# A transformer layer in exact fp32: unread products at the start, earlier weight tiles, and lower parts of weights made by an accumulating DMA

## The chip, the cores and the metric

The kernel runs on one core of one Trainium2 chip. The metric is the device time of one execution in microseconds (us). A core has TensorE (PE, matrix products, with a weight load that overlaps them), VectorE (DVE), ScalarE (ACT), GpSimd (POOL) and SyncE (SP). On-chip data lies in SBUF with 128 partitions; products land in eight banks of PSUM. Transfers from HBM are issued from a queue of an engine and moved by 16 DMA engines that the core's queues share.

## What is computed

One layer of a diffusion backbone for 512 latent tokens with a prefix of 256 context tokens, width 1024, all in fp32:

```python
mod = silu(c) @ w_ada + b_ada            # six vectors of 1024; the same for c_ctx
h  = rms_norm(x, g_norm1) * (1 + sc1) + sh1
hc = rms_norm(ctx, g_norm1) * (1 + csc1) + csh1
aq, ak, av, dq, dk, dv, dz, da, db, ga, gd = split_cols(h @ w_in)
...
y_attn = window_ctx_attention(q_a, k_a, v_a, k_ac, v_ac, attn_sink)
o_dl, _, _ = bidir_delta(*dn_inputs(dq, dk, dv, da, db), s_cf, s_cb)
...
y = sigmoid(gate_a) * (y_a @ w_br_attn) + sigmoid(gate_d) * (y_d @ w_br_dn)
x_new = x + gt1 * (y @ w_out)
x_new = x_new + gt2 * (square(relu(norm2(x_new) @ w_mlp1)) @ w_mlp2)
```

Here `y_d` is the normalised output of a bidirectional gated delta rule times `silu(dz)`, and `norm2` the second modulated RMS norm.

## The kernel before

**Precision.** Every weight product is made of three fast products. `split` and `wload` turn an fp32 operand into an upper part (a copy rounded to the fast type) and a lower part (operand minus upper part); `mm3` (L266) adds upper times upper, upper times lower, and lower times upper, on lines 271, 272 and 273, into one PSUM bank. `gate_tiles` (L925) and `br_a` (L970) do the same inline.

**Weight tiles.** A weight tile is 128 x 1024 (512 KB), that is 128 output columns with all eight blocks of 128 inputs; tiles of the branch projections (`wbr`) are half as large. `wload` issues the load on SP's queue into a ring of raw buffers, tag `wr`, of NWR = 4. ACT copies the raw tile to the upper part (L262), and DVE subtracts it from the raw tile for the lower part (L263). The parts go either into the rings `wh` and `wl` of NWS = 2 buffers each, or into buffers of a hand-managed arena (shown as `m` in the profile).

There are three groups of tiles.

- Three *early* tiles of `w_in`, with arena buffers. They are loaded within the loop over the eight blocks of x (`kt`): two at kt = 0 and one at kt = 1. After each block is normalised, the products of that block with all early tiles are issued, so these tiles advance as blocks become ready.
- Sixty *late* tiles: 36 of `w_in`, 16 of `wbr`, 8 of `w_out`, in a fixed list `wq`. `wnext` hands out the tile that was prepared and starts the load of the next, so one tile is prepared ahead. They use the rings `wh` and `wl`.
- Sixty-four MLP tiles, loaded by `wload` with arena buffers, far ahead of their use.

The raw ring is also used by `late_mod` (L988): 32 tiles `wa` of modulation weights, which DVE multiplies and sums on line 990, 16 of them between 379 and 440 us and 16 around the start of the MLP.

**The start.** SP's queue first carries x, the context and the 16 tiles of modulation weights `wada1` in 512 KB loads. `ada(kt)` (L190, products on L198) needs two of these; `columns(kt)` (L209) has ACT copy its result (L212), PE reduce it (L217) and DVE write the modulation of block kt. Meanwhile ACT squares and DVE sums x and the context, PE adds over partitions with a matrix of ones (L247), and ACT makes the reciprocal root. `modulate` (L275) then makes the upper and lower part of a normalised block: DVE on L276, ACT on L277, DVE on L278. The results stay on chip for all later input tiles.

**The stages after.** Input tiles are woven with attention (to about 300 us), the delta rule's chunks and their triangular solve (to about 440), gate tiles, the delta branch's projection (534 to 556), `w_out` (556 to 602) and the MLP (from 602). Generators written by hand set the order of instructions within each engine's queue; a helper library adds the semaphores, and each engine runs its queue in order.

Of the kernel before, what the change touches and what calls it, by code (L numbers as in the profile page):

```python
# [8 lines left out]
F32 = mybir.dt.float32  # L9
F32R = mybir.dt.float32r  # L10
BF16 = mybir.dt.bfloat16
AF = mybir.ActivationFunctionType
ALU = mybir.AluOpType
# [1 line left out]
PSUM = bass.MemoryType.PSUM  # L15

NU = 167
NWR, NWS = 4, 2
FILL = 144, 28, 36, (8, 7, 3)
INV = 2, 12, 18, 0  # L20
QTS = 7, 5, 4, 7, 3, 6, 10, 7
# [1 line left out]
LEAD = 0  # L23
ATT = 32
NHALF = 3
AHEAD = 2
LATE = 6, 3, 0
NPL = ()
# [3 lines left out]
P = 128  # L32
D = 1024
KT = D // P
# [17 lines left out]
T_AK, T_AV, T_AQ, T_AB = 0, 1, 2, 6  # L52
T_DK, T_DV, T_DQ, T_DZ = 7, 11, 15, 19
# [41 lines left out]
def tile_layer(ctx: ExitStack, tc: tile.TileContext, I: dict, out: bass.AP, dbg=None):  # L95
    nc = tc.nc
    V, A, G, PE = nc.vector, nc.scalar, nc.gpsimd, nc.tensor
# [4 lines left out]
    sb = ctx.enter_context(tc.tile_pool(name="sb", bufs=1))  # L102
# [3 lines left out]
    def nm(s):  # L106
        uid[0] += 1
        return f"{s}_{uid[0]}"
# [3 lines left out]
    banks = Arena(lambda o, n: psum[:, o:o + n], 512, 8)  # L112
# [4 lines left out]
    alloc, bank = mem.get, lambda n=1: banks.get(n * 512)  # L117
# [10 lines left out]
    r32 = lambda ap: ap.bitcast(F32R)  # L128
# [23 lines left out]
    ones = const.tile([P, P], F32, name="ones")  # L152
# [27 lines left out]
        (eng or V).tensor_tensor(r32(lo), src, hi, op=ALU.subtract)  # L180


    scb = alloc(256)
    scond = scb.ap.rearrange("p (k v) -> p k v", k=KT)
    V.memset(scb.ap, 0.0)
# [4 lines left out]
    def ada(kt):  # L190


        rp_ = banks.get(512, True)
        for half in range(2):
            wb = alloc(1024)
            nc.sync.dma_start(out=wb.ap, in_=I["wada1"][kt, half])
            for g in range(4):
                PE.matmul(rp_[32 * g:32 * g + 32, :256], scond[:, half * 4 + g], wb[:, g * 256:(g + 1) * 256],  # L198
                          start=(half == 0), stop=(half == 1))
            wb.free()  # L200
        return rp_
# [7 lines left out]
    def columns(kt, rp_):  # L209

        rb_ = alloc(256)
        A.activation(rb_.ap, rp_[:, :256], AF.Copy)  # L212
        rp_.free()
        mp_ = banks.get(512, True)
        mp = mp_[:, 0:4].rearrange("p (h n) -> p h n", h=2)
        for half in range(2):
            PE.matmul(mp[:, half, :], rb_[:, half * P:(half + 1) * P], prm[:, 184:186], start=True, stop=True)  # L217
        rb_.free()

        V.tensor_scalar(modA[:, kt, :], mp[:, 0, :], bada1[:, kt:kt + 1], g1[:, kt:kt + 1], op0=ALU.add, op1=ALU.mult)  # L220
        V.tensor_scalar(modS[:, kt, :], mp[:, 1, :], bada[:, kt:kt + 1], None, op0=ALU.add)
        mp_.free()

    columns(0, ada(0))
    for k4 in range(KT // 4):
        nc.sync.dma_start(out=cs_[:, k4 * 1024:(k4 + 1) * 1024], in_=I["ctxT"][k4])
    xt = [xs_[:, k * SEQ:(k + 1) * SEQ] for k in range(KT)]
    ct_ = [cs_[:, k * CTX:(k + 1) * CTX] for k in range(KT)]
    rstd = alloc(768)
# [2 lines left out]
    for src, nt, n, r in ((xs_, 4, SEQ, rx), (cs_, 2, CTX, rc)):  # L232
        tot = None
        for i in range(nt):
            b = alloc(1024)
# [6 lines left out]
        w = 512  # L242
# [9 lines left out]
        act(r, r, AF.Exp, scale=-0.5)  # L252


    def wload(src, n=KT, bufs=None):
        raw = sb.tile([P, KT, P], F32, tag="wr", bufs=NWR, name=nm("wr"))[:, :n]
        nc.sync.dma_start(out=raw, in_=src)
        if bufs:
            hi, lo = (b.ap.rearrange("p (k c) -> p k c", k=KT) for b in bufs)
        else:  # L260
            hi, lo = (sb.tile([P, KT, P], F32, tag=t, bufs=NWS, name=nm(t))[:, :n] for t in ("wh", "wl"))
        A.activation(r32(hi), raw, AF.Copy)  # L262
        V.tensor_tensor(r32(lo), raw, hi, op=ALU.subtract)  # L263
        return r32(hi), r32(lo)

    def mm3(acc, w, xs, start=True, stop=True, ks=None):  # L266
        ks = list(range(len(xs))) if ks is None else ks
        n = len(ks)
        for i, k in enumerate(ks):
            xhi, xlo = xs[i]  # L270
            PE.matmul(acc, w[0][:, k, :], xhi, start=(start and i == 0), stop=False)  # L271
            PE.matmul(acc, w[0][:, k, :], xlo, start=False, stop=False)  # L272
            PE.matmul(acc, w[1][:, k, :], xhi, start=False, stop=(stop and i == n - 1))  # L273

    def modulate(t, src, r, sc, sh, hi, lo, eng=V):  # L275
        V.scalar_tensor_tensor(t, src, sc, r, op0=ALU.mult, op1=ALU.mult)  # L276
        A.activation(r32(hi), t, AF.Identity, bias=sh)  # L277
        eng.scalar_tensor_tensor(r32(lo), t, sh, hi, op0=ALU.add, op1=ALU.subtract)  # L278
        return r32(hi), r32(lo)

    H, HCb = alloc(8 * 1024, True), alloc(8 * 512, True)
    hx, hc = [], []
    early, EARLY = [], {T_AB: 0, T_DK: 0, T_DK + 1: 1}
    ebufs = []
    for kt in range(1, AHEAD):
        columns(kt, ada(kt))
    for kt in range(KT):
        t = alloc(768)
        o, oc = kt * 1024, kt * 512
        hx.append(modulate(t[:, :512], xt[kt], rx, modA[:, kt, 0:1], modS[:, kt, 0:1],  # L290
                           H[:, o:o + 512], H[:, o + 512:o + 1024]))
        hc.append(modulate(t[:, 512:768], ct_[kt], rc, modA[:, kt, 1:2], modS[:, kt, 1:2],
                           HCb[:, oc:oc + 256], HCb[:, oc + 256:oc + 512]))
        t.free()
        if kt + AHEAD < KT:
            columns(kt + AHEAD, ada(kt + AHEAD))
        for t_, k0 in EARLY.items():
            if k0 == kt:
                bb = alloc(1024), alloc(1024)
                ebufs += bb  # L300
                early.append((wload(I["win"][t_], bufs=bb), bank(2)))
        for (w, acc), k0 in zip(early, EARLY.values()):
            for k in range(kt + 1) if kt == k0 else (kt,):
                mm3(acc[:, :512], w, [hx[k]], start=(k == 0), stop=(k == KT - 1), ks=[k])
                mm3(acc[:, 512:768], w, [hc[k]], start=(k == 0), stop=(k == KT - 1), ks=[k])
# [24 lines left out]
    for n in range(2):  # L330
# [5 lines left out]
    wq = [(I["win"][t], KT) for t in (T_DK + 2, T_DK + 3, T_AK, *range(T_AQ, T_AQ + 4), T_AV, *range(T_DV, T_DV + 4),  # L336
                                      *range(T_DQ, T_DQ + 4), *(t + i for t, i in gates[:ND1]))]
    wq += [(I["wbr"][0, ct], 4) for ct in range(8)] + [(I["win"][t + i], KT) for t, i in gates[ND1:]]
    wq += [(I["wbr"][1, ct], 4) for ct in range(8)] + [(I["wout"][ct], KT) for ct in range(8)]
    wq = [lambda a=a: wload(*a) for a in wq]  # L340
    wn = [wq.pop(0)()]

    def wnext():
        w = wn.pop()
        if wq:
            wn.append(wq.pop(0)())
        return w
# [249 lines left out]
    t, t2 = alloc(TOK), alloc(TOK)  # L597
# [386 lines left out]
    def late_mod(grp):  # L984

        for j in range(8):
            wa = sb.tile([P, KT, P], F32, tag="wr", bufs=NWR, name=nm("wa")).rearrange("p k c -> p (k c)")
            nc.sync.dma_start(out=wa, in_=I["wada2"][grp, j])  # L988
            t = alloc(1024)
            V.scalar_tensor_tensor(t.ap, wa, 0.5, scr.ap, op0=ALU.mult, op1=ALU.mult, accum_out=modT[:, grp, j:j + 1])  # L990
            t.free()
            if j == 7:
                V.tensor_tensor(modT[:, grp], modT[:, grp], bada[:, 16 + 8 * grp:24 + 8 * grp], op=ALU.add)
            yield

    late = (x for grp in range(4) for x in late_mod(grp))
# [143 lines left out]
    for g in range(2):  # L1140
        ms = slice(16 * g, 16 * g + 16)
        f, b = xa[0][:, ms], xa[1][:, ms]
# [9 lines left out]
    for g in range(2):  # L1152
# [12 lines left out]
        for a in range(2):  # L1165
            lo, hi = quad(a, 0), quad(a, 1)
# [37 lines left out]
    for qq in range(2):  # L1204
# [3 lines left out]
        for a in range(2):  # L1208
            n = 2 * qq + a
            t = alloc(512)  # L1210
# [15 lines left out]
    for ct in range(8):  # L1226
        w = wnext()
# [31 lines left out]

    for ct in range(8 - NHALF):  # L1260
        w = wnext()
# [9 lines left out]

    wlast = [wnext() for _ in range(NHALF)]
    accs = [bank() for _ in range(NHALF)]
    wfirst = []
# [16 lines left out]
    def load_first():  # L1291
        for i in range(NHALF):
            bufs = [alloc(1024), alloc(1024)]
            first.append([bufs, wload(I["wm1"][i], bufs=bufs)])
# [3 lines left out]
    for n, cols in enumerate(halves):  # L1298
        for i in range(NHALF):
            if n and i == NHALF - 1:  # L1300
                norm(halves[0])
# [20 lines left out]
    for hf in range(4):  # L1322
        act_ = []
        for f in range(FT):
            if first:
                bufs, _, acc = first.pop(0)
            else:
                bufs = [alloc(1024), alloc(1024)]
                w = wload(I["wm1"][hf * FT + f], bufs=bufs)
# [17 lines left out]
        for ct in range(8):  # L1347
            acc = bank()
            bufs = [alloc(1024), alloc(1024)]
            w = wload(I["wm2"][ct * 4 + hf], bufs=bufs)  # L1350
# [118 lines left out]
```

## Time and profile before

| | us |
|---|---|
| median of three runs | 962.74 |
| the three runs | 957.93, 962.74, 963.81 |
| profiled execution | 959.5 |
| span of its instructions | 957.7 |
| mean granted TensorE clock in it | 0.979 |

The profile is of one execution. Busy time is given for each engine; "PEld" is the weight load of PE, and a row "PE banks<-m,wh" is a product with an upper part of a late tile. A row of the timeline has a start, a duration, the engine, the line and the tiles, and in square brackets the idle time before it and what ended that. Matmuls overlap, so a row's duration is longer than the distance to the next row's start. "SPq" rows are issues of transfers. PEclk is the clock granted to TensorE, in parts of the full one.

The chain of work that ended last is, for the late part, PE alone:

```profile
PE 47%; DVE 0%; ACT 0%; POOL 0%; issue 0%; POOLq 0%
```

### The profile page before, as it was taken

The numbers are of one execution on the slowest core, as the hardware profiler recorded it, in microseconds if no ns is written. First come the engines' busy times: TensorE is split into PE (matmuls) and PEld (weight loads), VectorE is DVE, ScalarE is ACT, GpSimd is POOL, SyncE is SP. The second block draws the span as 40 slices with busy tenths as digits, with TensorE's granted clock in tenths as the row PEclk, the third lists the DMA queues.
The fourth block names the chain that finished last, engine by engine and source line by source line (L and its number), as shares of the span: only waits on it lengthen the run. The fifth ranks groups of instructions, "written<-read, shape, count | busy, mean of one in ns | idle before, by whom it ended". The sixth has DMA issues, their size and how long they took to land. (4 is left out here: it accounts for less than half of the span.)

```text
span 957.7 us, 18080 instructions
## 1 busy us (share of the span) xinstructions
PE 905.8 (95%) x7696; PEld 731.6 (76%) x7696; DVE 596.6 (62%) x994; ACT 444.7 (46%) x815; POOL 36.4 (4%) x45
## 2 busy tenths in 40 slices
PE   3999889999899999879999999999999999999998
PEld 1688667877677677658787879988888888888886
DVE  4666778997788899755577665982365225423511
ACT  5357634337567877337555433661154115313400
POOL 0001211000000000100011000000000000000000
PEclk9799989999999999889999999999999999999999
DMA  9721102110001133850123534381164213322101
GB/s 357 297 95 44 46 25 66 67 45 24 11 13 34 34 100 107 300 202 25 46 69 122 187 132 154 120 278 65 42 206 137 78 66 131 111 66 74 59 34 54
DMA packets 29601, 98.72 MB, mean 103 GB/s; under 512 B 3664, under 2 KB 4176, under 8 KB 29520
## 3 DMA queue, kind: packets, MB, share of 16 engines
q1 hardware_dynamic: 29520, 97.57, 29.6%
q8 instruction: 60, 0.98, 0.4%
q14 instruction: 21, 0.17, 0.0%
HBM read 95.46 MB, written 2.10 MB: 102 GB/s over the span
## 5 line engine op out<-in xcount | busy, mean ns | idle before, releaser
L271 PE MATMUL banks<-m,m 128*128 128x512 f32 (+1 forms) x584 | 219.8, 380 | 1.3 <-ACT m L277 1.3
L272 PE MATMUL banks<-m,m 128*128 128x512 f32 (+1 forms) x584 | 219.8, 378 | 0.0
L273 PE MATMUL banks<-m,m 128*128 128x512 f32 (+1 forms) x584 | 218.7, 378 | 0.8 <-DVE m L263 0.8
L262 ACT ACTIVATE m<-wr 128x1024 fp32r<-128x1024 f32 x67 | 71.1, 1062 | 149.8 <-PE banks L272 78.0
L271 PEld LDWEIGHTS banks<-m,m 128*128 128x128 f32 x584 | 109.7, 189 | 23.4 <-issue 3.1
L273 PEld LDWEIGHTS banks<-m,m 128*128 128x128 f32 x584 | 109.7, 189 | 22.0 <-DVE m L263 1.1
L272 PEld LDWEIGHTS banks<-m,m 128*128 128x128 f32 x584 | 110.1, 189 | 21.0 <-issue 0.8
L263 DVE TENSOR_TENSOR m<-wr,m 128x1024 fp32r<-128x1024 f32 x67 | 82.0, 1224 | 63.9 <-ACT m L262 34.8
L271 PE MATMUL banks<-m,wh 128*128 128x512 f32 (+1 forms) x312 | 114.3, 367 | 0.4 <-DVE m L537 0.4
L272 PE MATMUL banks<-m,wh 128*128 128x512 f32 (+1 forms) x312 | 112.2, 360 | 0.0
L273 PE MATMUL banks<-m,wl 128*128 128x512 f32 (+1 forms) x312 | 111.8, 359 | 0.0
L925 PE MATMUL banks<-m,wh 128*128 128x512 f32 x320 | 108.2, 413 | 0.0
L1352 DVE SCALAR_TENSOR_TENSOR m<-banks,modT,m 128x512 f32<-128x512 f32 x32 | 24.0, 750 | 104.0 <-PE banks L273 104.0
L262 ACT ACTIVATE wh<-wr 128x1024 fp32r<-128x1024 f32 (+1 forms) x60 | 56.6, 944 | 56.1 <-PE banks L272 23.9
L263 DVE TENSOR_TENSOR wl<-wr,wh 128x1024 fp32r<-128x1024 f32 (+1 forms) x60 | 64.7, 1078 | 22.6 <-ACT wh L262 22.3
L925 PEld LDWEIGHTS banks<-m,wh 128*128 128x128 f32 x320 | 61.7, 196 | 13.7
L925 PE MATMUL banks<-m,wl 128*128 128x512 f32 x160 | 67.3, 421 | 0.0
L271 PEld LDWEIGHTS banks<-m,wh 128*128 128x128 f32 x312 | 59.0, 189 | 9.5 <-DVE m L537 0.7
L272 PEld LDWEIGHTS banks<-m,wh 128*128 128x128 f32 x312 | 59.3, 190 | 9.0 <-issue 0.5
L273 PEld LDWEIGHTS banks<-m,wl 128*128 128x128 f32 x312 | 59.0, 189 | 8.7 <-DVE wl L263 0.3
L179 ACT ACTIVATE m<-m 128x512 fp32r<-128x512 f32 (+1 forms) x56 | 35.0, 630 | 47.5 <-DVE m L1335 19.9
L180 DVE TENSOR_TENSOR m<-m,m 128x512 fp32r<-128x512 f32 (+1 forms) x56 | 38.2, 689 | 20.9 <-ACT m L179 20.4
(229 smaller groups left out, 1293.3 us busy)
## 6 DMA issues: line engine op xcount, KB each, us to landing
wr<-in_wm SPq DMA_DIRECT2D x64, 512.0 KB, 3.5
wr<-in_win SPq DMA_DIRECT2D x39, 512.0 KB, 3.6
wa<-in_wada SPq DMA_DIRECT2D x32, 512.0 KB, 4.3
m<-in_wada SPq DMA_DIRECT2D x16, 512.0 KB, 10.2
m<-in_xT SPq DMA_DIRECT2D x8, 512.0 KB, 6.0
wr<-in_wbr SPq DMA_DIRECT2D x16, 256.0 KB, 2.7
wr<-in_wout SPq DMA_DIRECT2D x8, 512.0 KB, 3.7
out<-m SPq DMA_DIRECT2D x8, 256.0 KB, 2.0
```

Of the source, the lines that this page charges most:

```text
L179: A.activation(r32(hi), src, AF.Copy)
L180: (eng or V).tensor_tensor(r32(lo), src, hi, op=ALU.subtract)
L262: A.activation(r32(hi), raw, AF.Copy)
L263: V.tensor_tensor(r32(lo), raw, hi, op=ALU.subtract)
L271: PE.matmul(acc, w[0][:, k, :], xhi, start=(start and i == 0), stop=False)
L272: PE.matmul(acc, w[0][:, k, :], xlo, start=False, stop=False)
L273: PE.matmul(acc, w[1][:, k, :], xhi, start=False, stop=(stop and i == n - 1))
L925: PE.matmul(acc.ap, w[x][:, k, :], hx[k][y], start=(k == p == 0), stop=(k == KT - 1 and p == 2))
L1352: V.scalar_tensor_tensor(xn_[ct], acc.ap, modT[:, 3, ct:ct + 1], xn_[ct], op0=ALU.mult, op1=ALU.add)
```

## The change

Four things are changed together.

1. Before anything else on PE, NONES = 70 products of a 128 x 128 matrix of ones with itself go into a PSUM bank that nobody reads.
2. The early tiles are loaded sooner, one each: after the modulation of block 0 and the context loads, with the modulation of block 1, and at kt = 0. All three take part in the products from block 0 on.
3. For the sixty late tiles the lower part is made in another way: ACT copies the raw tile a second time with scale -1 into the lower part's buffer, rounded to the fast type like the upper part, and a DMA on GpSimd's queue then adds the source weights from HBM onto it. DVE's subtraction is gone for them. The early and the MLP tiles keep it.
4. NWR goes from 4 to 2, NWS from 2 to 3, and two tiles are prepared ahead in place of one (WAHEAD).

```diff
-NWR, NWS = 4, 2
+NWR, NWS = 2, 3
+WAHEAD = 2
...
+NONES = 70
...
+    wb_ = banks.get(512, True)
+    for _ in range(NONES):
+        PE.matmul(wb_[:, :P], ones, ones, start=True, stop=True)
+    wb_.free()
...
+    def wload(src, n=KT, bufs=None, late=False):
+
+        raw = sb.tile([P, KT, P], F32, tag="wr", bufs=NWR, name=nm("wr"))[:, :n]
+        nc.sync.dma_start(out=raw, in_=src)
...
+        A.activation(r32(hi), raw, AF.Copy)
+        if late:
+            A.activation(r32(lo), raw, AF.Copy, scale=-1.0)
+            G.dma_start(out=r32(lo), in_=src, accum_op=ALU.add)
+        else:
+            V.tensor_tensor(r32(lo), raw, hi, op=ALU.subtract)
+        return r32(hi), r32(lo)
+
+    early, EARLY = [], {T_AB: 0, T_DK: 0, T_DK + 1: 0}
+    ebufs = []
+
+    def load_early():
+        bb = alloc(1024), alloc(1024)
+        ebufs.extend(bb)
+        early.append((wload(I["win"][list(EARLY)[len(early)]], bufs=bb), bank(2)))
+
     columns(0, ada(0))
     for k4 in range(KT // 4):
         nc.sync.dma_start(out=cs_[:, k4 * 1024:(k4 + 1) * 1024], in_=I["ctxT"][k4])
+    load_early()
...
     for kt in range(1, AHEAD):
         columns(kt, ada(kt))
+        load_early()
...
-        for t_, k0 in EARLY.items():
-            if k0 == kt:
-                bb = alloc(1024), alloc(1024)
-                ebufs += bb
-                early.append((wload(I["win"][t_], bufs=bb), bank(2)))
+        if len(early) < len(EARLY):
+            load_early()
...
-    wq = [lambda a=a: wload(*a) for a in wq]
-    wn = [wq.pop(0)()]
+    wq = [lambda a=a: wload(*a, late=True) for a in wq]
+    wn = [wq.pop(0)() for _ in range(WAHEAD)]

     def wnext():
-        w = wn.pop()
+        w = wn.pop(0)
```

The old `wload` and its place in the file, ahead of `mm3`, are gone; the new one stands ahead of the first call of `columns`.

More of the change, by code (lines that the diff above doesn't have):

```diff
@@ L222, in columns @@
         mp_.free()
+    def wload(src, n=KT, bufs=None, late=False):
+        raw = sb.tile([P, KT, P], F32, tag="wr", bufs=NWR, name=nm("wr"))[:, :n]
+        nc.sync.dma_start(out=raw, in_=src)
+        if bufs:
+            hi, lo = (b.ap.rearrange("p (k c) -> p k c", k=KT) for b in bufs)
+        else:
+            hi, lo = (sb.tile([P, KT, P], F32, tag=t, bufs=NWS, name=nm(t))[:, :n] for t in ("wh", "wl"))
+        A.activation(r32(hi), raw, AF.Copy)
+        if late:
+            A.activation(r32(lo), raw, AF.Copy, scale=-1.0)
+            G.dma_start(out=r32(lo), in_=src, accum_op=ALU.add)
+        else:
+            V.tensor_tensor(r32(lo), raw, hi, op=ALU.subtract)
[6 more added lines that the diff above has]
+        early.append((wload(I["win"][list(EARLY)[len(early)]], bufs=bb), bank(2)))
     columns(0, ada(0))
@@ L252, in tile_layer @@
         act(r, r, AF.Exp, scale=-0.5)
[L255 to L264, printed above, removed]
     def mm3(acc, w, xs, start=True, stop=True, ks=None):
@@ L282, in tile_layer @@
     hx, hc = [], []
-    early, EARLY = [], {T_AB: 0, T_DK: 0, T_DK + 1: 1}
-    ebufs = []
     for kt in range(1, AHEAD):
         columns(kt, ada(kt))
+        load_early()
     for kt in range(KT):
```

## The prediction, made before the changed kernel ran

> **What bounds the kernel now.** I read the totals first, then windows along the span, then what TensorE (PE) waits for.
>
> ```profile
> PE 905.8 (95%) x7696; PEld 731.6 (76%) x7696; DVE 596.6 (62%) x994; ACT 444.7 (46%) x815; POOL 36.4 (4%) x45
> ```
>
> PE is busy for 95% of the span, so a change pays where PE stands idle or runs slowly. The windows (span piece, then busy time per engine, granted clock, DMA share and GB/s) show where that is.
>
> ```profile
> 20.06:33.71 13.65, 11.04 (x47) 7.02 (x48) 9.87 (x19) 6.64 (x12) 0.00 (x0) 0.50 1.03 410
> 34.00:64.70 30.70, 30.70 (x224) 24.21 (x224) 19.14 (x39) 11.54 (x20) 1.47 (x2) 1.00 0.37 132
> 200.00:220.00 20.00, 16.35 (x206) 11.92 (x205) 19.08 (x33) 11.34 (x26) 2.07 (x4) 1.00 0.09 28
> 300.00:320.00 20.00, 17.99 (x103) 13.64 (x101) 17.64 (x34) 18.99 (x38) 0.00 (x0) 1.00 0.10 28
> 379.00:441.00 62.00, 51.87 (x1308) 41.95 (x1306) 38.47 (x65) 29.66 (x59) 6.22 (x12) 0.86 0.60 206
> 660.00:900.00 240.00, 240.00 (x1060) 198.50 (x1059) 100.41 (x111) 72.06 (x88) 0.00 (x0) 1.00 0.29 97
> ```
>
> The MLP (660 to 900) is pure PE, and nothing can be won there. The start runs at half clock with the DMAs full. Around 200 VectorE (DVE) is nearly full while PE has gaps, around 300 ScalarE (ACT) is, and around 380 to 440 the DMAs and the clock are the weak place. PE's waits by releaser give the sizes:
>
> ```profile
> PE banks L684 <- issue: 11.3, 5, 3.4
> PE banks L198 <- DMA m<-in_wada: 11.1, 1, 11.1
> PE banks L684 <- DVE m L714: 2.4, 1, 2.4
> PE banks L472 <- DVE m L562: 2.4, 1, 2.4
> PE banks L513 <- DVE m L530: 1.2, 1, 1.2
> ```
>
> The first is inside a serial solve that the change leaves alone; the second is the wait for the first modulation weight. Waits that DVE ends are about 8 us over the whole span, the largest three being above. No wait on a late weight tile's lower part stands in the list.
>
> **The start: unread products and earlier weights.**
>
> ```profile
> 11.12 1.08 PE L198 MATMUL banks<-m,m 128*32 128x256 f32 x8 [11.12 <-DMA m<-in_wada]
> 26.77 0.79 PE L271 MATMUL banks<-m,m 128*128 128x512 f32 x1
> 27.36 0.63 PE L272 MATMUL banks<-m,m 128*128 128x512 f32 x1
> 34.02 0.64 PE L198 MATMUL banks<-m,m 128*32 128x256 f32 x8
> 56.28 0.40 PE L271 MATMUL banks<-m,m 128*128 128x512 f32 x1
> 56.52 0.40 PE L272 MATMUL banks<-m,m 128*128 128x512 f32 x1
> 64.68 0.40 PE L271 MATMUL banks<-m,wh 128*128 128x512 f32 x1
> 25.68 1.04 ACT L262 ACTIVATE m<-wr 128x1024 fp32r<-128x1024 f32 x1
> 20.91 0.75 DVE L278 SCALAR_TENSOR_TENSOR m<-m,modS,m 128x512 fp32r<-128x512 f32 x1
> 232.14 1.16 PE L536 MATMUL banks<-c_ident,st 128*128 128x128 f32 x8
> 233.14 0.71 PE L513 MATMUL banks<-c_ident,m 128*128 128x128 f32 x5
> ```
>
> Eight passes of 128 columns take 1.00 us from their start to the next row, 0.125 each. 70 fp32 products are 140 passes (the trace shows two for each fp32 product): 17.5 us, from 1 us on, and some 1 to 2 us more for passes at half clock at first. They end at 18.5 to 20. The first 11 us stood empty anyway, but the modulation products at 11.12 and the RMS sum behind them on PE's queue now start 7 us later. At full clock (0.64 against 1.08 per eight) they are through by about 21; the first normalised x, whose lower part ends at 21.7, becomes ready at about 23.7. The first weight's upper part, at 25.68 the last thing before the first product at 26.77, is made early now. So the three-product series begins at about 24.5.
>
> Between 26.77 and 34 the trace holds 10 long, 4 short and 16 modulation passes; at the later pace (0.24 from 56.28 to 56.52, half of it for the short ones, 0.08 as at 34.02) 4.1 us of work took 7.2. From 34 to 64.7 PE is full. The new end is 24.5 + 4.1 + 30.7 = 59.3 if nothing starves, and 58.5 with the smaller modulation share: a gain of 5.4 to 6.2, taken as **-6**. If the array stays warm throughout and the last modulation weights land as before, up to -9; if it falls back to half clock before 24.5, only the earlier start counts, 26.77 - 24.5 = -2.3. The three weights come ahead of later modulation tiles on SP's queue; the DMAs move the same bytes to about 38 us (410 GB/s above), and products of the first x blocks fill the shift.
>
> The Trainium skill, "TensorE: Matmul & The Clock Gate", Part 1, says that the array runs at half clock until about 3.4 us of sustained work, and drops again after idle time. The half-clock stretch above agrees (13.65 us is four times 3.41). By that rule the unread products alone do not suffice, as the pauses behind them can drop the clock again; that is the third rival.
>
> **The lower part by DMA.**
>
> ```profile
> L262 ACT ACTIVATE wh<-wr 128x1024 fp32r<-128x1024 f32 (+1 forms) x60 | 56.6, 944 | 56.1 <-PE banks L272 23.9
> L263 DVE TENSOR_TENSOR wl<-wr,wh 128x1024 fp32r<-128x1024 f32 (+1 forms) x60 | 64.7, 1078 | 22.6 <-ACT wh L262 22.3
> wr<-in_win SPq DMA_DIRECT2D x39, 512.0 KB, 3.6
> wr<-in_wbr SPq DMA_DIRECT2D x16, 256.0 KB, 2.7
> m<-in_wada SPq DMA_DIRECT2D x16, 512.0 KB, 10.2
> wa<-in_wada SPq DMA_DIRECT2D x32, 512.0 KB, 4.3
> q1 hardware_dynamic: 29520, 97.57, 29.6%
> ```
>
> DVE loses 60 subtractions, 64.7 us. Only what bounds PE counts: of the 8 us of PE waits on DVE, and gaps such as 200 to 220 (3.65 us of PE idle, DVE 19.08 of 20), I take half: **-4**, bounds -6 to 0, since what is late next there is the chain of small DVE steps itself. ACT gains 60 copies like the first row, 56.6 us. Mostly idle, it hides them, except around 300 to 320 (18.99 of 20): some five half-size wbr tiles lie about there, 0.6 us each (half of 1.05 and a little), half hidden: **+1.5**, bounds 0 to +4.
>
> No accumulating DMA is in this trace. From issue to landing a plain 512 KB tile takes 3.6, and 10.2 with the queues full; the second is the upper end, the first the lower one. I take 5 (3.6 plus reading the 512 KB once more at 410 GB/s, 1.3), nearer the lower, because the queues are at 29.6% on average; for 256 KB, 4, bounds 2.7 to 7.9.
>
> The Trainium skill, "DMA: Bandwidth & Descriptors", section "Anatomy of one DMA", gives about 2.0 us plus bytes at 436 GB/s for a GpSimd DMA: 3.2 us as an estimate. By it the two waits below would vanish and the sum be 2.5 us lower; it speaks of plain transfers, and no run here shows it.
>
> Where a late landing bites is read from the time between a tile's copies and its use:
>
> ```profile
> 54.83 0.39 ACT L212 ACTIVATE m<-banks 128x256 f32<-128x256 f32 x1 [1.29 <-PE banks L198]
> 57.20 1.12 ACT L277 ACTIVATE m<-m,modS 128x512 fp32r<-128x512 f32 x2 [1.04 <-DVE m L276]
> 547.79 0.39 PE L271 MATMUL banks<-m,wh 128*128 128x512 f32 x1
> 550.59 0.39 PE L271 MATMUL banks<-m,wh 128*128 128x512 f32 x1
> 553.65 1.04 ACT L262 ACTIVATE wh<-wr 128x1024 fp32r<-128x1024 f32 x1
> 556.19 0.39 PE L271 MATMUL banks<-m,wh 128*128 128x512 f32 x1
> ```
>
> *First late tile.* Its copies now lie on ACT behind the last modulate (58.3, that is 3.5 after the last column copy at 54.83) and two small copies of the triangle constants; with two copies of 1.05 the DMA goes out about 6.7 after the column copy. PE wants the lower part 10.3 after it (two products after 64.68, less 54.83). That leaves 3.65: **+1.3** for 5, +6.5 for 10.2, 0 for 3.6.
>
> *Second wbr run.* A tile takes 2.8 us (547.79 to 550.59). Upper and lower buffers come free three tiles back, so a load may start two tiles ahead: 5.6 + 0.47 - 1.26 of copies - 0.16 = 4.65 for 4. **0**; at 7.9 three tiles take 1.26 + 7.9 + 2.5 + 0.3 = 12.0 in place of 8.4, 1.2 each, +7 over six.
>
> *First wout tile.* Copies of 2.1 there leave 3.8: **+1.2**, at 10.2 +6.4. Later wout tiles last 5.6 and have 9.4. Elsewhere a tile lasts 5 us and more with two ahead, so over 8 are left. GpSimd's queue carries the issues in order between small steps (36.4 us in all), which I cost at nothing while they aren't late.
>
> **The raw ring of two.**
>
> ```profile
> 379.50 5.04 SPq L988 DMA_DIRECT2D wa<-in_wada  x4
> 387.61 9.35 SPq L988 DMA_DIRECT2D wa<-in_wada  x6
> 419.93 23.75 SPq L257 DMA_DIRECT2D wr<-in_win  x5
> DVE m L990 <- DMA wa<-in_wada: 11.4, 9, 4.0
> ```
>
> Weight tiles and late modulation tiles share it. From 379 to 425 some 17 to 22 loads go through; with two buffers each is held for 4.3 of landing plus some 1.2 on DVE or ACT, 2.75 per load: 47 to 60 us for 46 available. DVE waited 11.4 there already, off PE's path. I take **+1.5**, bounds 0 to +8. In the MLP a tile of 24 products lasts 5.4 us (240 us for 1060), so 2.75 per load hides: 0.
>
> **Sum**, on the profiled execution of 959.5 (span 957.7): -6 - 4 + 1.5 + 1.3 + 1.2 + 1.5 = -4.5, giving 955.0. The median of the three is 962.7, 3.2 above the profiled one, which lies inside their spread of 5.9; by the median the same sum gives 958. I take 956, as executions near the profiled one are as common as those near the median.
>
> **The rivals.**
>
> *All hidden.* Landings at 3.6 and less, ring and ACT covered, the start warm: -8 - 5 = -13, 946.5. For it: DMA share is low in most windows, and slack before use is mostly several us. Against: 379 to 441 at 0.60, and the reads of late tiles double.
>
> *Accumulations land late.* At about 10 us each: 6.5 + 7 + 6.4 at the three places, 1.6 on later wout tiles, about 7 at the tile used at 423 where three loads go out close together, 1.5 for ACT, less 10 for start and DVE: +20, 979. It decides from where the sum turns: each us above 5 costs 1 at each of the first, the wout and the 423 tile, so at 6.5 the -4.5 is gone. For it: a full DMA system does take 10.2. Against: in no late stage are the queues that full for long.
>
> *The clock falls back.* Only -2.3 at the start, the rest as summed: -0.8, 958.7.
>
> *The ring of two starves 379 to 441.* +8 to +15 in place of 1.5: +2 to +9, 962 to 969.
>
> **Chances and range.** Forecast 0.42 (946 to 964 by its own terms: the bounds of start and DVE below, of ACT and the ring above), all hidden 0.28, late landings 0.13, clock 0.08, ring 0.09. A change of this kernel is told from none at about 1%, 9.6 us: below 953.1 lies the second case and a fifth of the first, 0.37; above 972.4 the late landings and a little of the ring and of the forecast's tail, 0.18; within, 0.45. The range that holds 8 in 10 is 942 to 975: all of the forecast, nearly all hidden, the clock and the ring, and late landings only in part.
>
> **What would show it.** Half clock gone between 20 and 34, the first late tile's first product near 59 in place of 64.7, lower parts landing about 5 us from issue, no wait of PE on them but at the first late tile and the first wout tile of one to two us each, DVE down by about 65 us and ACT up by about 57. Wrong would be: PE waits on the lower parts that sum to over 10 us (late landings), or PE gaps of 8 us more from 379 to 441 (the ring), or 0.50 still standing from 20 to 34 (the clock).

## The result and the profile after

| | us |
|---|---|
| before, median of four runs | 962.12 (957.93 to 963.81) |
| changed, median of four runs | 1003.01 (1000.01 to 1009.21) |
| ratio | 1.044, 95% interval 1.038 to 1.050 |
| changed, profiled execution | 1002.51, span 1000.7 |

The change makes the kernel 41 us slower, outside the forecast's range. The totals, the DMA queues and the DMA issues (KB each, median us from issue to landing) of the changed kernel's page:

```profile
PE 930.5 (93%) x7836; PEld 755.4 (75%) x7836; DVE 545.8 (55%) x934; ACT 493.1 (49%) x875; POOL 86.5 (9%) x105
...
q1 hardware_dynamic: 29520, 97.57, 29.6%
q0 software_dynamic: 8640, 27.27, 16.1%
...
wl<-in_win POOLq DMA_DIRECT2D x36, 512.0 KB, 7.8
...
wl<-in_wbr POOLq DMA_DIRECT2D x16, 256.0 KB, 4.4
```

DVE is relieved by 51 us and ACT loaded by 48, less than the 65 and 57 that the prediction named as signs: busy time counts instructions that overlap once, and the 60 subtractions and the 60 new copies themselves are 64.7 and 56.1 us. The new line is the queue q0, the accumulating DMAs: 27.27 MB take 16.1% of the DMA engines' time, where 97.57 MB of plain loads take 29.6%. Per byte that is twice as much, and a 512 KB addition lands 7.8 us after its issue. What PE waits for, by releaser (total, times, longest):

```profile
PE banks L702 <- issue: 16.4, 5, 5.0
PE banks L295 <- DMA wl<-in_wout: 9.1, 3, 4.8
PE banks L803 <- ACT m L796: 6.5, 2, 3.3
PE banks L295 <- DMA wl<-in_win: 5.2, 1, 5.2
PE banks L943 <- DMA wl<-in_win: 5.0, 1, 5.0
PE banks L295 <- DMA wl<-in_wbr: 4.7, 2, 3.8
```

Lower parts that have not landed now stop PE for 24 us in all (before: none). L702 is the old L684, and its stalls without a named releaser have grown from 11.3 to 16.4. The 11.1 us wait for the first modulation weight is gone from the list, since the unread products fill it.

**Where the time went.** The table compares, stage by stage, with the kernel before (us, positive is slower). The first column ends where the first product of a late tile starts; every other stage ends with the last product that reads its last tile's lower part (in e5, where none does, its upper part). The late tiles are numbered 0 to 59 in order of use. Later runs stand beside it:

| run | until tile 0 | 0-1 | 2-29 | 30-35 | 36-45 | 46-51 | 52-53 | 54-59 | MLP | span |
|---|---|---|---|---|---|---|---|---|---|---|
| changed kernel | -3.5 | +8.2 | -1.0 | +16.9 | +3.3 | +7.0 | +5.0 | +7.3 | -0.1 | +43.0 |
| e2: rings alone | -0.4 | +0.2 | +0.6 | +0.1 | +0.6 | 0.0 | +0.4 | -0.6 | 0.0 | +0.9 |
| e3: overwriting DMA | -2.8 | +2.3 | -1.6 | +7.6 | +0.3 | +4.5 | +0.7 | +5.8 | +0.5 | +17.3 |
| e5: lower parts unread | -3.6 | 0.0 | +1.3 | +8.0 | +5.8 | 0.0 | +9.9 | +11.2 | +0.1 | +32.9 |
| e6: tiles 2-29 alone | -2.7 | +0.2 | +3.8 | -0.8 | -0.3 | 0.0 | +0.9 | -0.6 | +1.3 | +1.9 |
| e7: no unread products | -2.0 | +0.1 | +2.1 | +3.1 | 0.0 | 0.0 | 0.0 | 0.0 | 0.0 | +3.4 |
| e8: 42 unread products | -2.1 | +0.2 | -3.2 | -3.8 | 0.0 | 0.0 | 0.0 | -0.1 | 0.0 | -8.9 |
| e9: tiles 30-35 alone | -3.6 | +0.2 | +0.7 | +13.4 | +0.1 | 0.0 | +0.2 | -0.6 | +1.0 | +11.5 |
| e10: tiles 44-59 alone | -0.6 | +0.2 | +3.0 | +0.2 | +1.1 | +7.6 | +6.3 | +8.0 | +1.5 | +27.1 |

Each row is one profiled execution, and they differ by some us from execution to execution, above all in tiles 2 to 35; medians of several runs stand with the experiments. Tiles 0 and 1 are the first two, 30 to 35 the gate tiles beside the modulation loads, 44 to 51 the second wbr run, 52 to 59 `w_out`. The changed kernel loses most in tiles 0-1, 30-35, 46-51, 52-53 and 54-59. Three of these (0-1, 46-51 and 52-53) are the places that the prediction named for a late landing.

The first of them, in the timeline:

```profile
58.74 1.01 POOL L243 DMA_DIRECT2D wl<-in_win  x1 [58.28 <-ACT wl L242]
```

```profile
61.15 0.63 PE L293 MATMUL banks<-m,wh 128*128 128x512 f32 x2
61.62 0.40 PE L294 MATMUL banks<-m,wh 128*128 128x512 f32 x1
61.85 0.28 PE L293 MATMUL banks<-m,wh 128*128 128x256 f32 x1
61.97 0.51 PE L294 MATMUL banks<-m,wh 128*128 128x256 f32 x2
67.66 0.80 PE L295 MATMUL banks<-m,wl 128*128 128x512 f32 x1 [5.18 <-DMA wl<-in_win]
```

PE has issued all that needs no lower part by 62.48 and then stands still until 67.66, 8.9 us after the addition was issued. What follows is in the windows (columns as in the prediction):

```profile
66.80:73.60 6.80, 5.94 (x18) 4.97 (x19) 4.52 (x9) 4.40 (x6) 0.86 (x1) 0.50 0.70 160
379.00:455.00 76.00, 55.43 (x1262) 43.70 (x1260) 33.82 (x55) 34.77 (x58) 13.02 (x22) 0.84 0.66 180
414.80:428.40 13.60, 7.53 (x193) 6.24 (x187) 7.10 (x12) 5.82 (x10) 3.04 (x6) 0.51 0.48 162
455.60:462.40 6.80, 4.62 (x66) 3.98 (x66) 1.38 (x2) 1.70 (x7) 0.00 (x0) 0.53 0.72 203
568.40:572.00 3.60, 3.60 (x11) 2.78 (x10) 0.21 (x1) 0.59 (x2) 0.00 (x0) 0.53 0.97 273
```

From the last part of the 5.18 us of waiting on, the clock is 0.50 for 6.8 us, so the stall costs more than its length: tiles 0 and 1 lose 8.2. A stretch of half clock stands beside the waits that end at 457.78 and 567.78 too. In the mean over the span the granted clock fell from 0.979 to 0.967.

### The profile page after: what moved, and what is told of

It reads as the page before. It is cut to its first block, busy times and chain, and to the rows that moved or that the text cites. A ratio compares the mean times of both kernels' runs of the same rounds, so it can differ in the third digit from the quotient of the medians.

```text
span 1000.7 us, 18443 instructions
## 1 busy us (share of the span) xinstructions
PE 930.5 (93%) x7836; PEld 755.4 (75%) x7836; DVE 545.8 (55%) x934; ACT 493.1 (49%) x875; POOL 86.5 (9%) x105
## 3 DMA queue, kind: packets, MB, share of 16 engines
q1 hardware_dynamic: 29520, 97.57, 29.6%
q0 software_dynamic: 8640, 27.27, 16.1%
## 4 chain that ended last, share of the span: by engine, by line
PE 65%; issue 13%; DMA 7%; ACT 7%; DVE 6%; POOL 1%; POOLq 0%; DVEq 0%; ACTq 0%
PE banks L293 15%; PE banks L294 15%; PE banks L295 15%; PE banks L943 6%; DMA wa<-in_wada 3%; PE banks L988 2%; DMA wl<-in_win 2%; DMA wl<-in_wout 2%; PE banks L531 1%; PE banks L1054 1%; ACT wh L240 1%; ACT m L831 1%; PE banks L1085 1%; PE banks L537 1%; PE banks L702 1%
## 5 line engine op out<-in xcount | busy, mean ns | idle before, releaser
L295 PE MATMUL banks<-m,wl 128*128 128x512 f32 (+1 forms) x312 | 115.0, 370 | 19.0 <-DMA wl<-in_wout 9.1
L293 PE MATMUL banks<-m,wh 128*128 128x512 f32 (+1 forms) x312 | 116.7, 375 | 0.0
L294 PE MATMUL banks<-m,wh 128*128 128x512 f32 (+1 forms) x312 | 114.3, 367 | 0.0
L943 PEld LDWEIGHTS banks<-m,wh 128*128 128x128 f32 x320 | 61.7, 196 | 14.7 <-issue 1.0
L293 PEld LDWEIGHTS banks<-m,wh 128*128 128x128 f32 x312 | 61.4, 197 | 8.9 <-issue 0.2
L294 PEld LDWEIGHTS banks<-m,wh 128*128 128x128 f32 x312 | 61.3, 197 | 8.8 <-issue 0.2
L243 POOL DMA_DIRECT2D wl<-in_win x36 | 31.3, 870 | 329.5 <-ACT wl L242 293.9
L242 ACT ACTIVATE wl<-wr 128x1024 fp32r<-128x1024 f32 (+1 forms) x60 | 56.1, 935 | 0.1
L1008 DVE SCALAR_TENSOR_TENSOR m<-wa,m 128x1024 f32<-128x1024 f32 x32 | 39.7, 1246 | 29.2 <-DMA wa<-in_wada 28.8
```

The lines of the kernel that those rows point to most:

```text
L242: A.activation(r32(lo), raw, AF.Copy, scale=-1.0)
L243: G.dma_start(out=r32(lo), in_=src, accum_op=ALU.add)
L943: PE.matmul(acc.ap, w[x][:, k, :], hx[k][y], start=(k == p == 0), stop=(k == KT - 1 and p == 2))
```

## The experiments

All were compared with the kernel before in the same session; e1 to e4, e5 to e8 and e9 to e11 ran together.

**e1, the start alone.** Unread products and earlier early tiles; the rest as before.

```diff
-NWR, NWS = 2, 3
-WAHEAD = 2
+NWR, NWS = 4, 2
+WAHEAD = 1
...
-    wq = [lambda a=a: wload(*a, late=True) for a in wq]
+    wq = [lambda a=a: wload(*a) for a in wq]
```

> Parts 1 and 2 of the change alone: unread products and earlier early tiles; the late tiles and the rings as before. Both theories: the early phase ends 3 to 4 us sooner, as in the changed kernel (first late tile at 61.2 against 64.7), and nothing is given back: 958 to 959, ratio 0.996. If it comes out at 1.00 or above, the start itself costs something that the first trace hides.

Measured: 958.66 (950.63 to 964.77), ratio 0.996 [0.993, 1.000]. The start costs nothing and gains about 2.5 us, at the edge of its interval. Its profiled execution was a long one (964.77), and in it the clock fell after all:

```profile
26.70:33.50 6.80, 6.80 (x26) 5.17 (x27) 6.00 (x13) 3.07 (x5) 0.00 (x0) 0.50 1.03 408
```

**e2, the rings alone.** As the changed kernel, but lower parts by DVE's subtraction.

```diff
-    wq = [lambda a=a: wload(*a, late=True) for a in wq]
+    wq = [lambda a=a: wload(*a) for a in wq]
```

> The changed kernel with DVE's subtraction back in place of the second copy and the accumulating DMA; raw ring of two, three buffers for the parts, two tiles ahead. Theory 1 (the ring of two costs by itself, through DVE waiting on modulation tiles between 380 and 455): about 974, DVE waits on wa tiles still near 29 us. Theory 2 (accumulation and its traffic cost everything): 958 to 960, DVE waits on wa near 11.

Measured: 958.96, ratio 0.998 [0.995, 1.001]. Theory 1 falls on the time. DVE does wait longer for modulation tiles, between the two values expected, but PE does not feel it:

```profile
DVE m L1008 <- DMA wa<-in_wada: 21.8, 20, 3.0
```

It was 11.4 before. The wait is there and stays off the path; the ring of two, with the third buffer for each part and the second tile ahead, differs by 0.3 us from e1, well inside both intervals.

**e3, overwriting in place of adding.**

```diff
-            G.dma_start(out=r32(lo), in_=src, accum_op=ALU.add)
+            G.dma_start(out=r32(lo), in_=src)
```

> The changed kernel with the GpSimd DMA overwriting the lower part in place of adding to it, so the lower part is the whole weight; same bytes from HBM, same queue, same waits. Theory 1 with adding as the price: landing falls from 7.8 to 4 to 5 us, PE waits on lower parts from 24 to under 8 us, about 980. If the GpSimd queue is the price: landing stays above 7 and the time at 1003.

Measured: 975.74, ratio 1.014 [1.011, 1.017]. Queue and landings in this run's page, and PE's waits on lower parts:

```profile
q0 software_dynamic: 8640, 27.27, 8.0%
...
wl<-in_win POOLq DMA_DIRECT2D x36, 512.0 KB, 4.9
...
wl<-in_wbr POOLq DMA_DIRECT2D x16, 256.0 KB, 3.3
```

```profile
PE banks L295 <- DMA wl<-in_wout: 4.4, 2, 3.8
PE banks L295 <- DMA wl<-in_wbr: 2.7, 1, 2.7
PE banks L295 <- DMA wl<-in_win: 2.1, 1, 2.1
PE banks L943 <- DMA wl<-in_win: 0.6, 1, 0.6
```

The same packets and bytes take half the engine time, and the median landing of a 512 KB tile is 4.9 us, the 5 that the prediction had assumed. The waits fall from 24 to 9.8 us, not to the under 8 expected. So adding costs 27 of the 44 us between the changed kernel and e2. The other 17 come with the second copy and a second transfer through GpSimd's queue, even without adding. The median landing is not what counts there: where PE waits 2 us and more, the three transfers took 5.8, 6.9 and 6.8 us. The 7.6 us of tiles 30 to 35 have hardly a wait on a lower part in them (0.6), and no run splits them further.

**e4, modulation tiles out of the ring.**

```diff
-            wa = sb.tile([P, KT, P], F32, tag="wr", bufs=NWR, name=nm("wa")).rearrange("p k c -> p (k c)")
+            wb = alloc(1024)
+            wa = wb.ap
...
             t.free()
+            wb.free()
```

> The changed kernel with the 32 modulation tiles wa in arena buffers, so that the raw ring of two carries weight tiles alone. Theory 1: DVE waits on wa fall, the 19 us lost between 380 and 455 mostly return, about 986. Theory 2: about 1003.

Measured: 1002.12, ratio 1.041 [1.036, 1.046]. Nothing returns; tiles 30 to 35 still lose 14.1 us. With e2 this ends the theory that the ring's size costs.

**e5, lower parts that nobody waits for.**

```diff
             G.dma_start(out=r32(lo), in_=src, accum_op=ALU.add)
+            lo = hi
```

> The changed kernel in which the products of the late tiles take the upper part where they took the lower one (upper times x_hi stands for lower times x_hi); the second copy and the accumulating DMA still run, unread. Theory A (PE waiting on late lower parts, about 24 us, and the half clock that follows each such wait carry the loss): 965 or less, near 959, half-clock time after 40 us back under 30 us. Theory B (the additional DMA traffic, at twice the time per byte, delays the other loads between 380 and 455): 980 to 990, with the L803 and L702 stalls still there.

Measured: 992.60, ratio 1.032 [1.028, 1.036]. Neither number was met: theory A wanted 965 or less, theory B at most 990. PE's first wait is gone with its cost (tiles 0 and 1: 0.0). At the end of the list the wait has only moved, as the waits of ACT and of PE show:

```profile
ACT wl L242 <- DMA wr<-in_wout: 29.5, 8, 7.1
ACT wl L242 <- DMA wr<-in_win: 20.4, 10, 4.9
```

```profile
PE banks L294 <- ACT wh L240: 7.0, 2, 3.9
PE banks L294 <- ACT m L181: 5.6, 2, 3.9
```

ACT's second copy needs a buffer, and the buffer is held until the addition of three tiles before has landed. (The profile puts the wait down to a plain load; in the changed kernel this copy had no idle time, and the only new DMA that it can wait for here is the addition.) ACT runs in order, so the next upper part is late, and PE waits for that. A slow landing therefore costs through the buffers even where nobody reads the sum. In tiles 30 to 35 8.0 us are lost with no wait on a lower part at all, as theory B has it.

**e6, additions for tiles 2 to 29 alone.**

```diff
-    wq = [lambda a=a: wload(*a, late=True) for a in wq]
+    wq = [lambda a=a, n=n: wload(*a, late=2 <= n < 30) for n, a in enumerate(wq)]
```

> The changed kernel with the accumulating DMA for the late tiles 2 to 29 alone, where the tile is prepared 8 us and more ahead; the first two and all from 30 on keep DVE's subtraction. Theory A: no PE wait on a lower part; DVE's relief is worth something or nothing: 953 to 960. Theory B: half of the traffic remains, 965 to 975.

Measured: 956.22, ratio 0.995 [0.992, 0.998]. Landings are as slow as ever, but no PE wait on a lower part is left:

```profile
wl<-in_win POOLq DMA_DIRECT2D x20, 512.0 KB, 7.8
```

So the additions cost nothing that shows where the lead is long enough. e6 is 2.7 us faster than e2, which the relief of DVE would explain, but the two are from different sessions and their intervals overlap.

**e7 and e8, the parts of the start.** e7 has the earlier loads without unread products, e8 42 of them in place of 70; both with rings and late tiles as in e1.

```diff
-NONES = 70
+NONES = 42
```

> Early tiles loaded sooner, no unread products; late tiles and rings as before. If the unread products carry the start's gain (full clock to 26): about 961, ratio 1.00, half clock from 20 to 34 as before. If the earlier loads carry it: 957 to 959.

> As the run with the start alone, but 42 unread products, 84 passes of 0.125 us, which end at about 11.5, when the first modulation weight has landed. If delaying the modulation by 7 us is what limits the start's gain: 955 to 957. If the pause after the products lets the clock fall at once: 960 to 961, half clock from about 18 to 32.

Measured: e7 958.71, ratio 0.996 [0.993, 0.999]; e8 954.14, ratio 0.993 [0.990, 0.996]. The earlier loads alone gain what e1 gains, so the 70 products add nothing that shows in the medians. e8 is 4.6 us faster than e7 in the same session. First rows of e8, then of e7:

```profile
1.06 11.39 PE L187 MATMUL banks<-ones 128*128 128x128 f32 x84 [1.06 <-DVE ones L155]
12.38 0.64 PE L206 MATMUL banks<-m,m 128*32 128x256 f32 x8
```

```profile
18.50:25.30 6.80, 5.85 (x21) 1.90 (x21) 3.42 (x5) 1.48 (x3) 0.00 (x0) 0.51 1.02 405
```

```profile
20.06:33.71 13.65, 12.76 (x70) 7.84 (x70) 9.73 (x19) 6.41 (x11) 0.00 (x0) 1.00 1.03 409
```

```profile
26.55 1.08 PE L202 MATMUL banks<-m,m 128*32 128x256 f32 x8
29.43 0.64 PE L202 MATMUL banks<-m,m 128*32 128x256 f32 x8
```

In e8 PE runs at full pace from 12.38 on (0.64 us for eight modulation passes), and the clock falls from 18.4 to 25.2. For e7 the clock column reads 1.00, but the rows do not agree: eight passes still take 1.08 us at 26.55, as in the kernel before at 11.12, and 0.64 at 29.43. So e7, without unread products, runs at half pace until about 28, and the column does not show it. Even so the first late tile begins at 62.62 in e8 and at 62.65 in e7. What e8 gains beyond e7 does not lie in the start of these two traces but in tiles 2 to 35, where executions of one kernel differ as well (e8's trace is its fastest run, e7's its slowest). Why 42 products come out best is open.

**e9, additions for tiles 30 to 35 alone; e10, for tiles 44 to 59 alone.** Edits as in e6, with `30 <= n < 36` and `n >= 44`.

> The changed kernel with the accumulating DMA for the late tiles 30 to 35 alone, those used between 380 and 455; all others keep DVE's subtraction. If the 17 us that this stage lost come from its own six accumulations beside the modulation loads through the ring of two: 959 + 10 to 17, so 969 to 976. If that loss was carried in from the stages before (the stage merely meets them shifted): 958 to 961.

> The accumulating DMA for the late tiles 44 to 59 alone: the second branch projection and w_out. If the landing against the short lead of these tiles is what costs there, the loss of the changed kernel after 534 us, 7 + 5 + 7, comes back whole: 976 to 980. If it needs the rest of the change: under 968.

Measured: e9 971.88, ratio 1.011 [1.008, 1.015], which is e2 plus 12.9. e10 986.03, ratio 1.025 [1.022, 1.028], e2 plus 27.1, more than the 19 expected. In the table each loses nearly all of it in its own stage. With the 8 of the first tiles the three make 48, and the changed kernel is 44 above e2. PE's waits in e10:

```profile
PE banks L295 <- DMA wl<-in_wout: 10.2, 3, 4.9
PE banks L295 <- DMA wl<-in_wbr: 5.3, 2, 4.0
```

Here the waits are on the sums themselves. Between 379 and 470 us in e9 most are not; first e9, then e2:

```profile
PE banks L702 <- issue: 11.7, 3, 5.1
PE banks L803 <- ACT m L796: 6.0, 2, 3.8
PE banks L943 <- DMA wl<-in_win: 2.4, 1, 2.4
```

```profile
PE banks L803 <- ACT m L796: 6.3, 2, 4.1
PE banks L702 <- issue: 5.6, 3, 2.7
```

Six additions put 2.4 us of waiting on sums and 6.1 more on stalls of L702 without a named releaser. The clock over 379 to 455 is 0.83 in e9 against 0.93 in e2; that this makes up the rest of the 12.9 is an inference.

**e11, 42 products and additions for tiles 2 to 29.** The edits of e6 and e8 on the changed kernel.

> 42 unread products, earlier early tiles, accumulating DMA for tiles 2 to 29 alone, raw ring of two. If DVE's relief and the start add up: 954.1 (42 products) - 2.7 (difference of the run with tiles 2 to 29 and the run with the rings alone) = 951 to 952. If they don't: 954 to 957.

Measured: 953.08, ratio 0.992 [0.989, 0.994]. The lowest median of all, between the two ranges expected. It is faster than the kernel before and the changed one, and not to be told from e8 (954.14), so the relief of DVE on top of the better start is not shown.

## Why the prediction was wrong

**The step that failed** is the landing of an addition: "I take 5 ..., nearer the lower, because the queues are at 29.6% on average", and 4 for 256 KB. Measured are 7.8 us for 512 KB in the median, and 8.9, 8.1 and 7.9 at the three places where the prediction set the landing against a lead. In the stretch from 530 to 650 us of the changed kernel:

```profile
wl<-in_wout POOLq DMA_DIRECT2D x8, 512.0 KB, 7.9
...
wl<-in_wbr POOLq DMA_DIRECT2D x8, 256.0 KB, 5.7
```

The average load of the queues was the wrong ground: adding itself takes the DMA engines twice as long per byte (16.1% against 8.0% in e3). The prediction counted the additional read from HBM at full rate, 1.3 us, and nothing for adding. It also had two smaller steps wrong: it priced a stall by its length, without the half clock after it, and it put nothing for additions in tiles 30 to 35 and at the last `w_out` tiles. Landing alone is not the whole: e3, with a median landing of 4.9 us, is still 20 us above the forecast of 956.

The Trainium skill, "DMA: Bandwidth & Descriptors", section "Anatomy of one DMA", has a formula that gives an estimate of 3.2 us for 512 KB on GpSimd's path. Here a transfer through GpSimd's queue took 4.9 without adding and 7.8 with it, in the median and beside other loads; the measurement decides.

**The places were right, their prices were not.**

- *First late tile.* The lead of 3.65 us was right (62.48 - 58.74 = 3.74). With 8.9 for the landing the wait is 5.2, as the formula says; with the half clock behind it tiles 0 and 1 lost 8.2.
- *Second wbr run.* Forecast 0 with 4 us and a lead of 4.65. Tiles 46 to 51 lose 7.0, of which 5.5 at tile 46 alone: its addition took 8.1 us, PE had work for 4.3 of them.

```profile
559.65 0.86 POOL L243 DMA_DIRECT2D wl<-in_wbr  x1 [4.78 <-ACT wl L242]
...
567.78 0.50 PE L295 MATMUL banks<-m,wl 128*128 128x512 f32 x1 [3.84 <-DMA wl<-in_wbr]
```

- *First w_out tile.* Lead 3.8 by the forecast (4.6 in the trace), landing 7.9, wait 3.4, loss 5.0 where +1.2 was forecast.
- *Later w_out tiles* were forecast as safe with 9.4. They are, up to the last three: the products of these are split into halves and woven, so their first uses come within some us of each other. That was overlooked, and costs 7.3.
- *Tiles 30 to 35.* The prediction put the danger on the ring of two, at +1.5. The ring is innocent (e2, e4); the six additions are not (e9, +12.9). The sign that was to tell of the ring, 8 us more of PE gaps from 379 to 441, came all the same (51.87 us busy before, 43.68 after): a sign of that kind tells the place and not the cause.

**The rival "accumulations land late"** described what happened, at +20 for landings of 10 us. At 7.8 it was +43: its sum left out the clock after stalls, most of the last w_out tiles and most of tiles 30 to 35. Its sign, PE waits on lower parts of over 10 us, came (24). Its point of turning, 6.5 us, does not fit: in e3, with a median of 4.9, the kernel is already 14.5 us slower than before. Its chance of 0.13 rested on "in no late stage are the queues that full for long", which has no bearing on a transfer that is slow by itself.

**What held.** The raw ring: +1.5 forecast, 0.3 measured in e2. GpSimd's small steps do not delay the issues: 59 of the 60 additions go out within 0.7 us of the end of their copy. ACT's 56 us of copies cost nothing that shows in tiles 18 to 29 (+0.9). Of DVE's relief, forecast at -4 and scaled to 28 of 60 tiles about -1.9, e6 shows -2.7, with the reservation above. Its ground was read too low: PE's waits that DVE ends sum to 12.3 us before, not 8.

**The start** was forecast at -6; in the changed kernel the first late tile begins 3.5 us earlier, and e1 gains 2.5. In this one execution its parts, clock and first product, came out nearly as forecast:

```profile
20.06:33.71 13.65, 12.15 (x93) 7.62 (x94) 9.92 (x20) 8.60 (x16) 0.00 (x0) 1.00 1.03 408
```

```profile
25.34 0.97 PE L293 MATMUL banks<-m,m 128*128 128x512 f32 x4
```

The full clock was luck in part. Nine traces have 70 products: in six the clock held at the start, and the first late tile begins 2.7 to 3.6 us earlier; in three (e1, e2, e10) it was 0.50 for 6.8 us from about 26.5 on, and 0.4 to 0.6 are left. That was the rival of the falling clock, at 0.08.

The sum was 24.5 + 4.1 + 30.7 = 59.3. Its 4.1 was counted from merged rows; the single records before 34.02 are 8 long, 6 short and 8 modulation passes, 3.3 by the same prices, which gives 58.5. Measured, the series begins at 25.34, 0.8 later, and lasts to 61.15, 35.8 in place of 34.8: both together leave 3.5 of the 5.4. The -6 is more than any trace gained at the start. One thing was passed over, on SP's queue in the changed kernel:

```profile
10.42 1.61 SPq L204 DMA_DIRECT2D m<-in_wada  x2
19.18 0.33 SPq L235 DMA_DIRECT2D wr<-in_win  x1
19.55 8.89 SPq L204 DMA_DIRECT2D m<-in_wada  x10
```

The third early load needs a buffer of the ring of two and stands before ten modulation loads; nothing is issued on this queue from 12.03 to 19.18. In e1, with four buffers, the third early load goes out at 13.21 and the ten modulation loads from 14.48 on. The last of them goes out at 28.4 in the one and 28.8 in the other, so the stop costs nothing that can be seen here.

## What to carry to other kernels

Moving work from a compute engine to an accumulating DMA trades busy time that may be hidden for a latency that has to be hidden: compare the landing with the lead of each tile, place by place, and use it only where the lead is ample (tiles 2 to 29 here), not everywhere. Even there no gain was shown clear of noise. Price a PE stall with the half clock that follows it: here waits of 5.2, 3.8 and 3.4 us cost 8.2, 5.5 and 5.0. Split a change into parts before judging it: three of its parts together cost nothing (e2), and two of them, with 42 products in place of 70, gain 7 us (e8), hidden behind a fourth that cost 44.

## What the runs showed of the hardware

In the trace's records of single DMA packets of the changed kernel, a packet of 4096 bytes takes 328 ns (median) in the accumulating queue and 159 in the plain one. In e3, where GpSimd's queue overwrites, it takes 174 there.

The clock column missed a half clock that had stood since the start in two traces: it reads 1.00 in e7 from 20.06 to 33.71 and in the kernel before at 11.12, while eight modulation passes take 1.08 us there in place of 0.64. The rows' durations decide.

The stalls that the profile leaves without a releaser ("issue") lie mostly in series of very short products. In all thirteen traces each over 0.9 us ends 1.2 to 1.6 us after a 16 KB packet of the instruction queue has ended. In the changed kernel between 379 and 455 us:

```
packet of the instruction queue      PE resumes on L702
start 416.77, took 0.96 us           419.13, after 4.04 us idle
start 420.83, took 0.97 us           423.13, after 2.03 us idle
start 437.84, took 0.97 us           440.28, after 4.95 us idle
```

That suggests that PE there waits for its own instructions, and that additions, which keep the DMA engines busy, delay them. The longest such stall without an addition beside it is 2.7 to 4.1 us (3.4 before, 4.1 in e1, 2.7 in e2). With additions beside it, it is 5.0 in the changed kernel, 6.2 in e4, 6.0 in e6 and 5.1 in e9, but only 3.5 in e11. No run changed the instruction loads alone, so this stays argued and not shown.
